# First attention: queries and keys turned unsplit in f32, two token tiles to a bank, and split behind the turn

## The chip, the cores and the metric

The kernel runs on one core of one Trainium2 chip. The metric is the device time of one execution in microseconds (us). The core has five engines with instruction queues of their own: TensorE (PE in the profile, with its weight loads as PEld), VectorE (DVE), ScalarE (ACT), GpSimd (POOL) and SyncE (SP, which issues the DMAs here). Each engine works through its queue in order; semaphores make one engine wait for another.

## The reference

The reference is a trunk of two layers over 1024 latent tokens and 256 context tokens, with a model width of 1024. Layer 0 mixes tokens by neighbourhood attention (16 heads of 64), layer 1 by sliding-window attention; each ends with a gated ConvFFN. All arithmetic is float32. Only the head of the first attention matters here, which normalises queries and keys per head:

```
y = h @ w_qkv
q = rmsnorm(y[..., :D_MODEL].reshape(bsz, t, n_kv, N_HEADS // n_kv, HEAD_DIM), g_q)
kv = y[..., D_MODEL:]
k = rmsnorm(kv[..., :kv_w].reshape(bsz, t, n_kv, HEAD_DIM), g_k)
v = kv[..., kv_w:].reshape(bsz, t, n_kv, HEAD_DIM)
...
s = jnp.einsum('...qngd,...knd->...ngqk', q, k).astype(jnp.float32) * (HEAD_DIM ** -0.5)
```

Behind it the scores get a bias (latent keys only), a softmax over latent neighbourhood and context keys together, and are multiplied by v.

## The kernel before

One program builds all stages one after another: an opening (the first modulation, the first norm, the first products with the weights), the first attention (`na`), the first ConvFFN, the sliding-window attention and the second ConvFFN. A product in f32 precision is made of f32r products: an operand is split into a high half (its rounding to f32r) and a low half (the remainder), and high x high, high x low and low x high are added up in one PSUM bank.

**The order of the work.** Each stage is planned before it is written out. `Sched.op` (line 237) records a step with its engine (or a choice of two), a planned length, what it reads and writes, a priority `key`, and which buffers it takes (`acq`) and gives back (`rel`). `Sched.run` plays the steps through in planned time, taking on each engine the ready step of lowest key; the order found is then issued, and every engine's queue stands in that order. Two tables correct the keys: `KINDS` by the name of the step, `RANKS` by its number in the plan. Waits that the plan doesn't know of are added when the steps are written out: the layer that places the semaphores makes two engines take turns on one PSUM bank, also where both only read.

**The first attention** works on eight head pairs. For each pair, `plan_na_qkv` (line 1339) is called for ten token tiles of 128 in the order 8, 9 (context) and 0 to 7 (latent). Its steps before the change, per tile:

- `plan_qkv_mm` (line 678): 24 matmuls of 384 columns (`mm<-whi,...`) give q, k and v of two heads; the first six tiles are made in the opening.
- `cp` (ACT) copies the 384 columns out of PSUM; `plan_rstd` (line 695) makes 1/rms of the four 64-wide heads, with one pow on POOL.
- `qn` (DVE) multiplies q and k by it; `qg` (POOL or DVE) multiplies q by `gg`, the product of both gains and the score's factor.
- `kd` and `qhi` (ACT) round k and q to f32r, k written twice; `klo` (DVE) and `qlo` (POOL or DVE) make the remainders. They fill a 512-column tile `st`; the k remainders go to `klt`, one for two token tiles.
- `tr` (PE) turns the four 128-column blocks of `st` in f32r into one PSUM bank of tag `pt`; `qev` (ACT), then `kev` (DVE or ACT) copy the q and the k half out. `kev` reads what `qev` wrote in the plan, so it stands behind it.
- On odd tiles `trl` (PE) turns the two blocks of `klt` into another `pt` bank, and `lev` (ACT) copies it out with two 64-partition reads.

So two token tiles take ten turns and three `pt` banks. There are two `pt` banks, used in rotation; the turns of the softmax weights (`pt<-idr,S`) take the same ones.

`plan_na_su` (line 1455) takes two query tiles of one head through scores (`s<-kkc,q`, `s<-kkl,q` and the low halves `klc`, `kll`), softmax (`S`), turns, splits (`pthi`) and the product with v (`pv<-pthi,v`). The score matmul has 128 rows: 64 of the high and 64 of the low half of q, against a k tile that holds the high half twice, plus a second k tile with the low half and 64 rows of zeros.

In the opening, `plan_quarter` (line 1101) makes a quarter of the modulation from weights `wm` that arrive by DMA (steps `mm`, `cp`, `tr`, `fin_`), and `apply` (line 1230) applies it and splits the result (`h0hi`, `h0lo`), which the first weight products wait for.

Of the kernel before, what the change touches and what calls it, by code (L numbers as in the profile page):

```python
# [38 lines left out]
class InOrder:  # L39
# [7 lines left out]
    def __getattr__(self, name):  # L47
        f = getattr(self.eng, name)

        def call(*a, **k):  # L50
# [11 lines left out]
    open=dict(load=-6, mm=1.7, tr=-9.6, fin_=0.4, sq=-9.9, v=-4.1, newton=-8.6, dg=-5.3, bc=5, lof=-6.8, mod=1.9),  # L62
    na=dict(f=0.3, cp=0.6, sq=-4.2, pw=2.2, vhi=0.2, vlo=3.3, qg=-1, kd=-0.9, qhi=-6.5, klo=0.7, qlo=-7, qev=-2, kev=-3.4,
          trl=-3.3, lev=-3.4, mm=-0.1, ctx_part=3.1, exp=0.2, hi=-0.5, lo=0.5, add=-5.5, load=-0.9, lat_part=-0.5,
          rec=2.9, ev=-0.1, scale=2.2, fin_=4.1),
# [8 lines left out]
    open={0: 0.9, 1: 21.9, 3: 18.2, 4: 28.9, 5: 11.3, 6: -19.6, 7: -0.2, 9: 3.8, 10: 1.6, 12: 31.4, 13: 32.6,  # L74
# [16 lines left out]
    na={36: 1, 47: -1.7, 48: 28.4, 50: 3, 54: 15.2, 57: 45, 61: -45.2, 62: -1.7, 67: 1.3, 68: 3.8, 69: 0.6, 71: -25,  # L91
# [304 lines left out]
def trunk_kernel(ctx, tc, xperm, xtok, xseq, cc, wmod0, wmod, bmod, gnorm, na_wqkv, na_gq, na_gk, na_bias, na_wo,  # L396
# [118 lines left out]
    def t_dve(n):  # L515
        return 0.065 + n / 960.0
# [822 lines left out]
    def plan_na_qkv(n):  # L1339
# [43 lines left out]
        def qg(e):  # L1383
            ENG[e].tensor_tensor(out=J["qn"][:, 0:2], in0=J["qn"][:, 0:2], in1=gg.unsqueeze(1).to_broadcast([P, 2, DH]),
                                 op=ALU.mult)
# [1767 lines left out]
```

## Time and profile before

| | us |
|---|---|
| median of 3 runs | 2743.69 (2743.62 to 2746.39) |
| profiled execution, its own time | 2744.96 |
| span of the profiled execution | 2743.0 |
| PE, DVE, ACT, POOL busy in the span | 2713.1, 2269.0, 1696.2, 389.3 |

The opening lasts to about 74 us, where the first turn of `st` starts; the last one of the first attention ends near 660 us, and its last head pair's softmax near 700 us. A group row names line, engine, operation, output and inputs, shapes and count, then busy time and the mean length of one in ns, then the idle time before it and what ended that. Nearly all rows carry line 51, the helper that records every instruction, so groups are told apart by the tile names. A matmul's record lasts longer than its place in the stream, since matmuls are pipelined: what one costs on PE is read from the distance between starts in the timeline.

### The profile page before, as it was taken

To read this page: it belongs to the slowest core of one execution; us is meant where nothing else is said; L and a number is where in the kernel's file an instruction comes from. 1 tells how busy PE (TensorE), PEld (TensorE's weight loads), DVE (VectorE), ACT (ScalarE), POOL (GpSimd) and SP (SyncE) were. 2 spreads that over 40 slices of the span, in tenths; PEclk is the share of its full clock that TensorE was granted. 3 is DMA by queue.
4 is the path that set the end of the run, shared out by engine and by line. 5 is a ranking of instruction groups with operands and counts; after the bars stand their busy time and mean duration, and the time that the engine had idled before them with its cause. 6 is when DMAs were issued, how large, how long until landed. Compare 5 with 4: busy or idle time off the path is not lost.

```text
span 2743.0 us, 44478 instructions
## 1 busy us (share of the span) xinstructions
PE 2713.1 (99%) x15615; PEld 2399.7 (87%) x15615; DVE 2269.0 (83%) x4860; ACT 1696.2 (62%) x3349; POOL 389.3 (14%) x649
## 2 busy tenths in 40 slices
PE   7999999999999999999999999999999999999999
PEld 6999999999899987788888889999988888888887
DVE  5878778889789677798998699888987989888766
ACT  5877777778556554455554458888864655545443
POOL 1211121224000000000000015556430000000000
PEclk9999999999999999999999999999999999999999
DMA  7233323334746544444577561010263234334745
GB/s 288 68 97 115 112 88 117 117 105 132 257 148 189 182 160 152 154 156 140 161 230 242 172 212 57 13 38 19 83 200 131 73 116 150 119 114 144 260 147 192
DMA packets 153108, 387.41 MB, mean 141 GB/s; under 512 B 23356, under 2 KB 38708, under 8 KB 151476
## 3 DMA queue, kind: packets, MB, share of 16 engines
q1 hardware_dynamic: 152884, 384.56, 43.2%
q8 instruction: 123, 2.02, 0.3%
q14 instruction: 101, 0.83, 0.1%
HBM read 313.46 MB, written 71.04 MB: 140 GB/s over the span
## 4 chain that ended last, share of the span: by engine, by line
PE 72%; DVE 2%; issue 1%; ACT 1%; DMA 0%; SPq 0%; DVEq 0%; ACTq 0%
PE ua L51 17%; PE dn L51 15%; PE uc L51 13%; PE mm L51 7%; PE ud L51 4%; PE oacc L51 4%; PE pt L51 3%; PE pv L51 3%; PE s L51 2%; PE dnc L51 2%; PE u L51 1%; PE mod L51 0%; DVE wlo L51 0%; DVE S L51 0%; PE bc L51 0%
## 5 line engine op out<-in xcount | busy, mean ns | idle before, releaser
L51 ACT ACTIVATE whi<-wraw 128x512 fp32r<-128x512 f32 (+1 forms) x264 | 213.0, 808 | 181.8 <-PE uc L51 54.3
L51 DVE TENSOR_TENSOR wlo<-wraw,whi 128x512 fp32r<-128x512 f32 (+1 forms) x264 | 240.8, 914 | 39.9 <-ACT whi L51 39.4
L51 ACT ACTIVATE S<-S,m 128x640 f32<-128x640 f32 (+3 forms) x288 | 221.0, 768 | 32.4 <-DVE m L51 25.8
L51 PE MATMUL dn<-ghi,whi 128*128 128x512 f32 x616 | 240.2, 390 | 0.0
L51 PE MATMUL dn<-ghi,wlo 128*128 128x512 f32 x616 | 240.0, 390 | 0.0
L51 PE MATMUL dn<-glo,whi 128*128 128x512 f32 x616 | 239.9, 389 | 0.0
L51 ACT ACTIVATE pthi<-pt 128x512 fp32r<-128x512 f32 (+2 forms) x384 | 195.5, 524 | 60.7 <-PE pt L51 38.3
L51 DVE SCALAR_TENSOR_TENSOR u<-c,cv,u 128x1023 f32<-128x1023 f32 x176 | 222.3, 1281 | 3.4 <-ACT u L51 2.9
L51 ACT ACTIVATE whi<-s 128x1024 fp32r<-128x1024 f32 (+1 forms) x116 | 109.0, 940 | 164.6 <-PE uc L51 111.0
L51 ACT ACTIVATE ghi<-graw 128x512 fp32r<-128x512 f32 x154 | 96.4, 630 | 176.5 <-PE dn L51 102.2
L51 PE MATMUL pt<-idr,S 128*128 128x128 f32 x1280 | 192.9, 273 | 1.6 <-DVE pthi L51 1.1
L51 PE MATMUL mm<-whi,h0hi 128*128 128x384 f32 x480 | 169.8, 354 | 0.0
L51 DVE TENSOR_TENSOR glo<-graw,ghi 128x512 fp32r<-128x512 f32 x154 | 105.6, 690 | 72.6 <-ACT ghi L51 66.9
L51 PEld LDWEIGHTS pt<-idr,S 128*128 128x128 f32 x1280 | 152.3, 141 | 13.7 <-DVE pthi L51 1.4
L51 PE MATMUL mm<-wlo,h0hi 128*128 128x384 f32 x480 | 161.7, 337 | 0.0
L51 PE MATMUL pv<-pthi,v 128*128 128x256 f32 (+1 forms) x560 | 153.2, 354 | 2.4 <-DVE pthi L51 1.5
L51 POOL TENSOR_TENSOR qy<-qv,mhalf 128x4 f32<-128x4 f32 (+1 forms) x112 | 121.3, 1084 | 210.2 <-DVE qv L51 193.2
L51 DVE TENSOR_TENSOR wlo<-s,whi 128x1024 fp32r<-128x1024 f32 (+1 forms) x116 | 124.5, 1076 | 23.0 <-ACT whi L51 22.7
L51 DVE TENSOR_TENSOR pthi<-pt,pthi 128x512 fp32r<-128x512 f32 (+2 forms) x208 | 117.9, 582 | 24.8 <-ACT pthi L51 23.0
L51 POOL TENSOR_TENSOR n1y<-n1v,mhalf 128x4 f32<-128x4 f32 (+1 forms) x8 | 8.9, 1113 | 905.8 <-DVE n1v L51 905.8
L51 PEld LDWEIGHTS dn<-ghi,whi 128*128 128x128 f32 x616 | 115.7, 188 | 24.0
L51 PEld LDWEIGHTS dn<-glo,whi 128*128 128x128 f32 x616 | 115.7, 188 | 23.9
(404 smaller groups left out, 8733.1 us busy)
## 6 DMA issues: line engine op xcount, KB each, us to landing
wraw<-in_w_up_dram SPq DMA_DIRECT2D x132, 512.0 KB, 4.2
wm<-in_wmod_dram SPq DMA_DIRECT2D x80, 512.0 KB, 3.9
wraw<-in_w_down_dram SPq DMA_DIRECT2D x44, 512.0 KB, 4.3
graw<-g_dram SPq DMA_DIRECT2D x44, 512.0 KB, 4.8
wraw<-in_w_down_dram SPq DMA_DIRECT2D x88, 256.0 KB, 3.2
graw<-g_dram SPq DMA_DIRECT2D x66, 256.0 KB, 2.9
slab<-in_na_wqkv_dram SPq DMA_DIRECT2D x32, 384.0 KB, 3.2
woraw<-in_na_wo_dram SPq DMA_DIRECT2D x24, 512.0 KB, 5.0
```

The source lines that it names most:

```text
L51: r = f(*a, **k)
```

## The change

`tr` now turns the normalised q and k themselves, in f32 and not yet split, two token tiles at once: q of both tiles in columns 0 to 255 of one `pt` bank, k of both in 256 to 511. The split is made from that bank, head by head, each step on 64 partitions and 256 columns:

- `qh` (ACT) writes the rounded q, times `gg` as a factor per partition; `ql` (DVE) writes the remainder to the other 64 partitions.
- `kh` (ACT) writes the rounded k; `kx` (ACT or POOL, SBUF to SBUF) copies it to the other 64 partitions; `kl` (DVE) writes the remainder.

The steps `qg`, `kd`, `qhi`, `klo`, `qlo`, `qev`, `kev`, `trl` and `lev` are gone, and so are the tiles `st` and `klt`. `gg` is one column. `qn` has four buffers instead of two; q tiles hold two token tiles, in half as many buffers. The gains come as one column from the host. `KINDS` and `RANKS` of the opening and of the first attention have new values; from the first ConvFFN on, the order on every engine is as it was.

```diff
-        sc.op("dve", t_dve(256), qn, reads=[K("raw"), K("y")], writes=[K("qn0"), K("qn1")], key=key,
-              acq=[("qn", K("qn"), 4)], rel=[K("raw")])
...
-            act.activation(J["kd"], J["qn"][:, 2:4].unsqueeze(2).to_broadcast([P, 2, 2, DH]), AF.Copy)
...
-            pt = J["pt"] = psa("pt", F32R)
-            for i in range(4):
-                pe.transpose(pt[:, i * P:(i + 1) * P], J["st"][:, i * P:(i + 1) * P], idr)
-        sc.op("pe", 0.35, tr, reads=[K("ql"), K("qh"), K("kd")], writes=[K("pt")], key=key, acq=[("pt", K("pt"), 2)],
-              rel=[K("st"), K("st")])
...
+        if tt % 2 == 0:
+            return
...
+            pt = J["pt"] = psa("pt", F32)
             for i in range(4):
+                src = f["qn", tt - 1 + i % 2]["qn"][:, i // 2 * 2:i // 2 * 2 + 2]
+                pe.transpose(pt[:, i * P:(i + 1) * P], src.rearrange("p h d -> p (h d)"), idf)
+        before = ("q0", hp, tt - 1)
+        sc.op("pe", 0.436, tr, reads=[K("qn"), before + ("qn",)], writes=[K("pt")], key=key, acq=[("pt", K("pt"), 8)],
+              rel=[K("qn"), before + ("qn",)])
+        for h2 in range(2):
+            r, x = ql_rows[h2], ql_rows[1 - h2]
...
+                act.activation(f["q"][pr][r, h2, :], J["pt"][r, 0:256], AF.Copy, scale=gg[r, :])
...
+                dve.scalar_tensor_tensor(out=t[x, h2, :], in0=J["pt"][r, 0:256], scalar=gg[r, :], in1=t[r, h2, :].bitcast(F32),
+                                         op0=ALU.mult, op1=ALU.subtract)
...
+                copy(e, kh_t()[r, h2, pair_cols], J["pt"][r, 256:512])
...
+                copy(e, kh_t()[x, h2, pair_cols], kh_t()[r, h2, pair_cols].bitcast(F32))
+            sc.op(("act", "pool"), (t_act(256), t_pool(256)), kx, reads=[kt("kh", h2)], writes=[kt("kx", h2)], key=key)
...
+                dve.tensor_tensor(out=kl_t()[r, h2, pair_cols], in0=J["pt"][r, 256:512],
+                                  in1=kh_t()[r, h2, pair_cols].bitcast(F32), op=ALU.subtract)
```

**On PE, in the stage's middle.** This is a piece of PE's queue before, where tiles of the second latent half (`n1lo`) are projected; `st` and `klt` are the split q and k and the k remainders:

```order
L51 MATMUL pt<-idr,st 128x128 x4
L51 MATMUL s<-kkc,q 128x256
L51 MATMUL s<-klc_697,q 128x256
L51 MATMUL s<-kkc,q 128x256
L51 MATMUL s<-klc_697,q 128x256
L51 MATMUL mm<-whi,h0hi_135 128x384
L51 MATMUL mm<-whi,n1lo 128x384
L51 MATMUL mm<-wlo,h0hi_135 128x384
L51 MATMUL pt<-idr,klt 128x128 x2
```

And this is a piece of it now, at such a place; `qn` is the normalised, unsplit q and k:

```order
L51 MATMUL pt<-idr,qn 128x128 x4
L51 MATMUL mm<-whi,h0hi_135 128x384
L51 MATMUL mm<-whi,n1lo 128x384
L51 MATMUL mm<-wlo,h0hi_135 128x384
L51 MATMUL pt<-idr,S 128x128 x4
L51 MATMUL pv<-pthi,v 128x512 x2
```

Ten turns for two token tiles have become four; over the whole program the turns of `st` fall from 496 to 176 and those of `klt` from 112 to 32 (what is left belongs to the second attention), and 160 turns of `qn` are new.

**On ACT and DVE, behind the turn.** ACT before, with buffer numbers; `pt_6154` is a bank of `st` blocks, `pt_6166` one of k remainders:

```order
L51 ACTIVATE q_6164<-pt_6154 128x256
L51 ACTIVATE kkl_694<-pt_6154 128x2x128
L51 ACTIVATE kll_695<-pt_6166 64x256 x2
L51 ACTIVATE S_6074,rs0_5578<-S_6074,m0_6075 128x640
L51 ACTIVATE st_6195<-qn_6183 128x256
```

ACT now, with the engines that each row waits for; `pt_7189` holds two token tiles:

```order
L51 ACTIVATE kkl_694<-pt_7189 64x256 [waits PE_49]
L51 ACTIVATE q_7203<-pt_7189,gg_692 64x256
L51 ACTIVATE kkl_694<-kkl_694 64x256 [waits Activation_49]
L51 ACTIVATE pthi_7212<-pt_7194 128x2x256 [waits PE_49]
L51 ACTIVATE q_7203<-pt_7189,gg_692 64x256 [waits DVE_49]
L51 ACTIVATE kkl_694<-pt_7189 64x256
```

and DVE now, on the same bank:

```order
L51 TENSOR_TENSOR kll_695<-pt_7189,kkl_694 64x256 [waits PE_49,Activation_49]
L51 SCALAR_TENSOR_TENSOR q_7203<-pt_7189,gg_692,q_7203 64x256
L51 TENSOR_SCALAR S_7223,m0_7224<-s_7207 128x256 [waits PE_49]
L51 TENSOR_TENSOR pthi_7212<-pt_7194,pthi_7212 128x2x256 [waits Activation_49]
L51 SCALAR_TENSOR_TENSOR q_7203<-pt_7189,gg_692,q_7203 64x256 [waits Activation_49]
L51 TENSOR_TENSOR kll_695<-pt_7189,kkl_694 64x256
```

The bank is now read eight times, by ACT, DVE, ACT and DVE in turn: the second q read of ACT waits for DVE's first two reads, and DVE's last two wait for it. Such a wait of ACT for DVE stands on 39 of the 40 pairs of tiles; before there was none on q.

**On DVE, in the opening.** Before, between the turned input tiles (`x_125`, from PSUM banks `nps` and `pv`) and the first high half `h0hi`; `modc` is the modulation, `wlo` a low half of the weights:

```order
L51 COPY x_125<-nps 128x512
L51 TENSOR_TENSOR wlo<-slab,whi 128x768
L51 TENSOR_TENSOR modc<-mod,bmod_t 128x2x2
L51 TENSOR_TENSOR modc<-mod,modc 128x2x2
L51 TENSOR_TENSOR modc<-mod,bmod_t 128x2x2
L51 TENSOR_TENSOR modc<-mod,modc 128x2x2
L51 SCALAR_TENSOR_TENSOR modc<-modc,gn 128x2x2
L51 TENSOR_TENSOR wlo<-slab,whi 128x768
L51 TENSOR_SCALAR x_125<-x_125,modc 128x512
L51 CAST h0hi_130<-x_125 128x512
```

And now:

```order
L51 TENSOR_TENSOR modc<-mod,bmod_t 128x2x2
L51 TENSOR_TENSOR modc<-mod,modc 128x2x2
L51 TENSOR_TENSOR modc<-mod,bmod_t 128x2x2
L51 TENSOR_TENSOR modc<-mod,modc 128x2x2
L51 SCALAR_TENSOR_TENSOR modc<-modc,gn 128x2x2
L51 TENSOR_SCALAR x_125<-x_125,modc 128x512 x2
L51 TENSOR_SCALAR x_123<-x_123,modc 128x256
L51 CAST h0hi_130<-x_125 128x512
L51 CAST h0chi<-x_123 128x256
L51 TENSOR_TENSOR h0lo_131<-x_125,h0hi_130 128x512 x2
```

One copy and two `wlo` no longer stand ahead of the first `h0hi`; the two `wlo` come behind `h0lo`.

More of the change, by code (lines that the diff above doesn't have):

```diff
@@ L61 @@
 KINDS = dict(
[L62 to L65, printed above, removed]
+    open=dict(load=-0.7, mm=-6.4, cp=0.6, tr=-3.7, fin_=-5.6, sq=4, v=-2.5, newton=4.7, dg=2.3, bc=0.5, lof=-10.6,
+          mod=-1.6),
+    na=dict(eps=-3.7, f=0.3, cp=-1, sq=-2.5, vhi=10, vlo=2.9, ql=-11.4, kl=0.1, mm=-0.1, ctx_part=5.2, exp=1.3, hi=-0.5,
+          lo=0.5, pvm=-1.3, add=-11.1, load=-1, lat_part=-0.5, rec=3.4, ev=0.1, scale=9.4),
     ffn0=dict(),
@@ L1325, in trunk_kernel @@
     F = {}
-    sc = Sched(dict(CAPS, klt=1))
+    sc = Sched(dict(CAPS, qn=4, q=4, qc=1))
     op0 = Oproj(sc, 0, 2, TC, psa, [("q0", HP - 1, tt, "acc") for tt in range(NT)],
@@ L1362, in vhi @@
             copy(e, vt[:, :, 0:DH], pair(J["raw"][:, 256:384]))
-        vk, qk = ("v", hp, tt), ("q", hp, tt)
+        vk = ("v", hp, tt)
         sees = 2 if cx else sum(1 for su in range(4) if any(tt in NA_SEES[2 * su + k] for k in range(2)))
@@ L1393, in plan_na_qkv @@
-        sc.op("act", t_act(256), kd, reads=[K("qn1")], writes=[K("kd")], key=key, acq=[("st", K("st"), 2)],
-              rel=[K("qn")])
-        def qhi(e):
-            J["qhi"] = J["st"][:, 0:384].rearrange("p (e d) -> p e d", d=192)[:, :, 0:DH]
-            act.activation(J["qhi"], J["qn"][:, 0:2], AF.Copy)
-        sc.op("act", t_act(128), qhi, reads=[K("qn0"), K("kd")], writes=[K("qh")], key=key, rel=[K("qn")])
-        kp = ("klt", hp, tt // 2)
-        def klo(e):
-            if tt % 2 == 0:
-                f["klt", tt // 2] = wk.tile([P, 2, P], F32R, tag="klt", name="klt", bufs=1)
-            ENG[e].tensor_tensor(out=pair(f["klt", tt // 2][:, tt % 2, :]), in0=J["qn"][:, 2:4],
-                                 in1=J["kd"][:, :, 0, :].bitcast(F32), op=ALU.subtract)
@@ L1407, in plan_na_qkv @@
-        sc.op("dve", t_dve(128), klo, reads=[K("qn1"), K("kd")] + ([kp] if tt % 2 else []), writes=[kp], key=key,
-              acq=[("klt", kp, 1)] if tt % 2 == 0 else (), rel=[K("qn")])
-        def qlo(e):
-            ENG[e].tensor_tensor(out=pair(J["st"][:, DH:DH + P]), in0=J["qn"][:, 0:2], in1=J["qhi"].bitcast(F32),
-                                 op=ALU.subtract)
-        sc.op(("pool", "dve"), (t_pool(128), t_dve(128)), qlo, reads=[K("qn0"), K("qh")], writes=[K("ql")], key=key,
-              rel=[K("qn")])
+        sc.op("dve", t_dve(256), qn, reads=[K("raw"), K("y")], writes=[K("qn")], key=key,
+              acq=[("qn", K("qn"), 1)], rel=[K("raw")])
@@ L1416, in tr @@
+        f["qn", tt] = J
+        if tt % 2 == 0:
+            return
+        pr = tt // 2
+        ql_rows = [slice(0, DH), slice(DH, P)]
+        q, kz = ("q", hp, pr), ("kz", hp % 2 if cx else 2)
+        kt = lambda x, e: (x + "c", hp, e) if cx else (x, pr, e)
+        pair_cols = slice(0, TC) if cx else slice(pr * TC, (pr + 1) * TC)
+        kh_t = lambda: f["kkc"] if cx else kkl
+        kl_t = lambda: klcs[hp % 2] if cx else kll
         def tr(e):
-            pt = J["pt"] = psa("pt", F32R)
+            pt = J["pt"] = psa("pt", F32)
@@ L1435, in plan_na_qkv @@
-        sc.op(("dve", "act"), (t_dve(256), t_actp(256)), kev, reads=[K("pt"), qk] + ([kk] if tt == 9 else []), writes=[kk],
-              key=key, acq=[("kkc", kk, 20)] if tt == 8 else (), rel=[K("pt")], port=False)
-        if tt % 2:
-            def trl(e):
-                pl = J["pl"] = psa("pt", F32R)
-                for i in range(2):
-                    pe.transpose(pl[:, i * P:(i + 1) * P], f["klt", tt // 2][:, i, :], idr)
-            sc.op("pe", 0.17, trl, reads=[kp], writes=[K("pl")], key=key, acq=[("pt", K("pl"), 1)], rel=[kp])
-            def lev(e):
-                f["klc"] = klcs[hp % 2]
-                dst = f["klc"] if cx else kll[:, :, (tt - 1) * P:(tt + 1) * P]
-                for e2 in range(2):
-                    copy(e, dst[e2 * DH:(e2 + 1) * DH, e2, :], J["pl"][e2 * DH:(e2 + 1) * DH, :256].bitcast(F32))
-            sc.op("act", 2 * t_actp(256), lev, reads=[K("pl"), ("kz", hp % 2 if cx else 2)], writes=[("klc", hp)] if cx else [("kl", tt - 1), ("kl", tt)],
-                  key=key, acq=[("klc", ("klc", hp), 20)] if cx else (), rel=[K("pl")])
+                src = f["qn", tt - 1 + i % 2]["qn"][:, i // 2 * 2:i // 2 * 2 + 2]
@@ L1469, in plan_na_su @@
         units = []
-        reads = [("kkc", hp), ("klc", hp)] + [("q", hp, 2 * su + k) for k in range(2)]
+        reads = [(x + "c", hp, e) for x in ("kh", "kx", "kl")] + [("q", hp, su, x, e) for x in "hl"]
         for k in range(2):
@@ L1473, in plan_na_su, with get @@
             ch = NA_SEES[tt] if tt < 8 else ()
-            def get(tt=tt, ch=ch):
-                q = f["q"][tt]
-                u = dict(q=q[:, e, :], kkc=f["kkc"][:, e, :], klc=f["klc"][:, e, :], sink=None)
+            def get(tt=tt, ch=ch, k=k):
+                q = f["q"][su][:, e, k * P:(k + 1) * P]
+                u = dict(q=q, kkc=f["kkc"][:, e, :], klc=klcs[hp % 2][:, e, :], sink=None)
                 if tt < 8:
@@ L1483, in get @@
                 return u
-            units.append(dict(nl=len(ch) * P, sink=0, get=get, rel_c=[("q", hp, tt), ("kkc", hp), ("klc", hp)],
-                              rel_l=[("q", hp, tt)],
+            units.append(dict(nl=len(ch) * P, sink=0, get=get, rel_c=[("q", hp, su), ("kkc", hp), ("klc", hp)],
+                              rel_l=[("q", hp, su)],
                               mask_key=[("bias", hp, e, (0, 0, 1, 1, 1, 1, 2, 2)[tt])] if tt < 8 else []))
-            reads += [("kk", c) for c in ch] + [("kl", c) for c in ch]
+            reads += [(x, c, e) for c in sorted({c // 2 for c in ch}) for x in ("kh", "kx", "kl")]
         def val(c):
@@ L3101, in layout @@
     rows = lambda g: np.broadcast_to(g, (P, g.shape[-1]))
-    a["na_gq"], a["na_gk"] = rows(i["na_g_q"][0]), rows(i["na_g_k"][0])
+    a["na_gq"], a["na_gk"] = [np.concatenate([g, g])[:, None] for g in (i["na_g_q"][0], i["na_g_k"][0])]
     idx = _na_bias_index()
```

52 lines of the change are left out of this document (26 added, 26 removed), and 184 rows, old and new, of tables (na, open).

## The prediction

> **What bounds the kernel now.** I first read the busy shares of the page, then a table of stretches, then PE's timeline. The first row says that PE is busy nearly all the time, but a busy PE is not yet a PE that sets the time.
>
> ```profile
> PE 2713.1 (99%) x15615; PEld 2399.7 (87%) x15615; DVE 2269.0 (83%) x4860; ACT 1696.2 (62%) x3349; POOL 389.3 (14%) x649
> ```
>
> The stretches of the opening and of the first attention show more. The columns are the stretch, its length, then the busy time of PE, PEld, DVE, ACT and POOL, the granted clock of PE, and the DMA share.
>
> ```profile
> core 0: us, PE busy (x) PEld busy (x) DVE busy (x) ACT busy (x) POOL busy (x), PEclk, DMA share, GB/s
> 28.00:33.00 5.00, 0.42 (x4) 0.22 (x3) 3.42 (x11) 3.60 (x6) 0.00 (x0) 0.77 1.04 418
> 33.00:41.00 8.00, 6.61 (x20) 6.21 (x21) 3.56 (x14) 2.44 (x5) 1.01 (x1) 0.50 1.02 424
> 41.00:75.00 34.00, 32.76 (x255) 28.76 (x255) 28.94 (x84) 20.01 (x42) 7.35 (x11) 1.00 0.45 156
> 100.00:660.00 560.00, 559.96 (x3815) 526.73 (x3814) 464.79 (x1583) 428.38 (x1138) 115.02 (x153) 1.00 0.35 107
> 660.00:700.00 40.00, 36.51 (x268) 33.29 (x267) 36.96 (x93) 33.73 (x70) 17.22 (x13) 1.00 0.61 191
> ```
>
> From 100 to 660 us, where the changed steps run, PE lacks 0.04 us of being busy throughout. DVE has 560 - 464.8 = 95 us to spare there, ACT 132 us. So PE sets the pace of this stretch: matmuls taken off its queue shorten it, as long as the others go on delivering in time. From 660 to 700 us DVE is the fuller one (37 of 40 us); no turn of q or k stands there any more.
>
> **The change part by part.** *The turns.* What a turn costs on PE is read from starts in the timeline (start, length, operation):
>
> ```profile
> 307.48 0.34 PE L51 MATMUL mm<-wlo,h0hi 128*128 128x384 f32 x1
> 307.65 0.46 PE L51 MATMUL pt<-idr,st 128*128 128x128 f32 x4
> 307.95 0.41 PE L51 MATMUL mm<-whi,h0hi 128*128 128x384 f32 x1
> 308.19 0.34 PE L51 MATMUL mm<-whi,n1lo 128*128 128x384 f32 x1
> ...
> 309.84 0.34 PE L51 MATMUL mm<-wlo,h0hi 128*128 128x384 f32 x1
> 310.02 0.28 PE L51 MATMUL pt<-idr,klt 128*128 128x128 f32 x2
> 310.13 0.41 PE L51 MATMUL mm<-whi,h0hi 128*128 128x384 f32 x1
> 310.38 0.34 PE L51 MATMUL mm<-whi,n1lo 128*128 128x384 f32 x1
> 310.56 0.34 PE L51 MATMUL mm<-wlo,h0hi 128*128 128x384 f32 x1
> 310.73 0.60 PE L51 MATMUL pt<-idr,S 128*128 128x128 f32 x4
> 311.08 0.42 PE L51 MATMUL mm<-whi,h0hi 128*128 128x384 f32 x1
> 311.34 0.34 PE L51 MATMUL mm<-whi,n1lo 128*128 128x384 f32 x1
> ```
>
> Two `mm` follow each other at 0.18 us (310.38 to 310.56). From the `mm` ahead of a group of turns to the second `mm` behind it lie two such steps and the group. Four `st` turns: 308.19 - 307.48 - 0.36 = 0.35 us. Two `klt` turns: 310.38 - 309.84 - 0.36 = 0.18 us. Four turns of `S`, which are f32 blocks of 128 x 128 as the new turns of `qn` are: 311.34 - 310.56 - 0.36 = 0.42 us. The stage has 80 tiles, so 80 groups of `st` and 40 of `klt` go, and 40 groups of `qn` come: 80 x 0.35 + 40 x 0.18 - 40 x 0.42 = 28.0 + 7.2 - 16.8 = **18.4 us less on PE**. An f32 turn is dearer than an f32r one (0.105 against 0.088 us), but there are 160 of them for 400.
>
> The records themselves last longer, 273 ns for a turn of `S`, since they overlap:
>
> ```profile
> L51 PE MATMUL pt<-idr,S 128*128 128x128 f32 x672 | 100.8, 273 | 1.1 <-DVE pthi L51 1.1
> L51 PE MATMUL pt<-idr,st 128*128 128x128 f32 x320 | 37.5, 241 | 0.0
> L51 PE MATMUL pt<-idr,klt 128*128 128x128 f32 x80 | 12.2, 234 | 0.0
> ```
>
> The Trainium skill ("TensorE: Matmul & The Clock Gate", Part 4, PE-mode transpose) gives about 275 ns for such a turn in a kernel's context, mostly access latency. The trace agrees on the record (273 ns), but its starts show that only 0.105 us of it holds the queue up. By the page's figure as a cost, 240 turns fewer would give 66 us, an estimate that I don't use.
>
> *VectorE and ScalarE.* The groups that go, and the nearest to those that come:
>
> ```profile
> L51 ACT ACTIVATE st<-qn 128x256 fp32r<-128x256 f32 x79 | 32.6, 412 | 12.8 <-DVE qn L51 11.6 <-PE pt L51 0.9
> L51 ACT ACTIVATE q<-pt 128x256 fp32r<-128x256 f32 x80 | 30.1, 378 | 17.3 <-PE pt L51 16.7
> L51 ACT ACTIVATE st<-qn 128x128 fp32r<-128x128 f32 x80 | 24.3, 304 | 1.0 <-POOL qn L51 0.4 <-DVE qn L51 0.3
> L51 ACT ACTIVATE kll<-pt 64x256 fp32r<-64x256 f32 x64 | 24.0, 374 | 2.0 <-PE pt L51 1.3
> L51 DVE TENSOR_TENSOR klt<-qn,st 128x128 fp32r<-128x128 f32 x79 | 22.8, 290 | 4.6 <-ACT st L51 3.9 <-PE pt L51 0.2
> L51 DVE TENSOR_TENSOR osb<-pv,pvup 64x256 f32<-64x256 f32 x79 | 32.7, 414 | 1.6
> L51 DVE CAST kkl<-pt 128x256 fp32r<-128x256 f32 x23 | 9.7, 423 | 7.7 <-ACT q L51 7.4
> ```
>
> DVE loses 205 passes over 128 x 128 (80 of `klt`, 68 of `qg`, 57 of `qlo`) at 0.290 us and 29 casts at 0.423 us, 71.7 us in all. It gains 160 reads of a bank on 64 partitions; the nearest row is `osb`, 0.414 us, so 66.2 us. That leaves DVE about level (-5 us). ACT loses 80 x (0.412 + 0.304), 131 bank reads of 128 x 256 (80 of q, 51 of k) at 0.378 and 80 on 64 partitions at 0.374, together 136.7 us. It gains 160 bank reads at 0.374 and 71 copies SBUF to SBUF at 0.412 at most, together 89 us: 48 us lighter. POOL loses 35 small passes and gets nine copies of `kx`, on an engine with 445 us idle of 560. None of this is on the path while PE is full, and no engine becomes fuller, so these terms count nothing.
>
> *The bank behind the turn.* Here work is added to a path. The bank is read by ACT, DVE, ACT, DVE in turn, and each waits with its own queue held up behind it: on ACT the exponentials and `pthi`, on DVE the score passes, on which the turns and `pv` of PE wait. While ACT waits, DVE makes two reads, 2 x 0.414 = 0.83 us; then DVE waits for one of ACT's, 0.374 us. Per pair of tiles at most 1.2 us is exposed, against 40 x 1.2 = 48 us in all; at least nothing is, where `kx`, `pthi` or score passes stand between. The next but one turn on PE needs this bank again, and other matmuls of PE fill that time. The `CAST kkl` row above is the nearest to such a wait: 23 such reads behind ACT's q read waited 7.4 us, 0.3 us each, and PE missed nothing by it. I take +2 us, and 0 to 16 us (0.4 us on each of 40 pairs) for the range.
>
> *The opening.* PE stands idle ahead of the first weight product:
>
> ```profile
> 33.14 0.69 PE L51 MATMUL s<-whi,h0hi 128*128 128x384 f32 x1 [4.72 <-DVE h0hi L51]
> 35.08 0.69 PE L51 MATMUL s<-whi,h0lo 128*128 128x384 f32 x1 [1.25 <-DVE h0lo L51]
> ```
>
> ```profile
> 29.73 0.96 DVE L51 TENSOR_TENSOR wlo<-slab,whi 128x768 fp32r<-128x768 f32 x1 [1.47 <-ACT whi L51]
> 30.60 0.16 DVE L51 TENSOR_TENSOR modc<-mod,bmod_t 128x4 f32<-128x4 f32 x1
> 31.33 0.96 DVE L51 TENSOR_TENSOR wlo<-slab,whi 128x768 fp32r<-128x768 f32 x1
> 32.21 0.54 DVE L51 TENSOR_SCALAR x<-x,modc 128x512 f32<-128x512 f32 x1
> ```
>
> The chain that ends in `h0hi` holds two `wlo`, each taking 0.87 us to the next start. Both move behind `h0lo`, which saves 1.7 us if the inputs of `modc` are there that early. The most is the whole idle time, 6.0 us; but the weights for the next quarter come over DMA queues that are full until 41 us (share 1.02), so PE may only wait later. If a second gap held the clock at 0.50 as from 33 to 41 us, 8 us at half speed would cost up to 4 us. I take -2.5 us, with -5 to +4 us. The small rest (which softmax passes go to ACT in the last 40 us, where DVE is full) I put at 0, with 2 us either way.
>
> *The sum.* -18.4 - 2.5 + 2.0 = -18.9 us. The profiled execution took 2744.96 us (span 2743.0 and 1.96 around it), so 2726.1 by it. It lies 1.3 us above the median of the runs, 2743.69; from that, **2724.8 us**.
>
> **The rivals.**
>
> *Part of the gain is given back at the bank* (chance 0.13). If the turns in rotation catch up with the bank, so that PE waits a further 0.25 us at each of 40 pairs, 10 us go: 2734.8. For it speaks the new taking of turns, which the plan's lengths don't hold; against it, that ACT has 48 us less to do. The Trainium skill ("PSUM — Partial Sum Buffer", PSUM bank collisions raise a hardware error) says that two engines must be kept apart on one bank and quadrant, reads against reads too: the wait can't be dropped. The casts' 7.4 us agree that one read stands behind the other.
>
> *Slower: the hand-over lands on PE in full* (0.05). If all 1.2 us per pair reach PE, +48 stands in place of +2: 2743.7 - 20.9 + 48 = 2770.8. It decides against the change from (18.4 + 2.5) / 40 = 0.52 us of PE wait per pair. DVE's 95 us and ACT's 132 us to spare speak against it.
>
> *No change* (0.07). DVE and ACT might in truth set the pace, with PE's order merely cut to it: then the freed time becomes waits of PE, 2743.7. DVE's 83% in the stretch speaks against it; that part of its idle time is waiting, which can't be filled, speaks for it.
>
> *A turn costs what its record lasts* (0.02): 320 x 0.241 + 80 x 0.234 - 160 x 0.273 = 52.2 us less, 2689 with the other terms. The starts above contradict it.
>
> That the change doesn't do what it says can't be: PE's queue holds 160 turns of `qn` and 400 turns fewer of the others.
>
> **How the numbers follow.** The forecast (PE's 18.4 us stay gained) has 0.73, and its own range is 2716 to 2732: from -18.4 - 5 - 2 with a few us for the turns' reading, to a loss of up to 8 us at the bank. The range reaches on to 2736 to take in the given-back case: 0.69 of the forecast's chance and 0.11 of that one make 0.8. A measurement of this kernel can tell 0.2%, 5.5 us, from no change. Faster by more: 0.73 + 0.13 + 0.02 = 0.88; within it 0.07; slower 0.05.
>
> **What would show it.** Right: PE still busy throughout between the first turn of `qn` and the last, with this stretch some 18 us shorter; four turns of `qn` at about 0.42 us by starts; DVE's busy time there level, ACT's some 45 us less; PE's first `h0hi` product some 2 us earlier. Wrong: waits of PE's turns for DVE `kll` or `q`, or of its score products for DVE `q`, of more than 0.4 us per pair; a second idle gap of PE ahead of 50 us with the clock at 0.5; or 64-partition reads that take much longer than 0.414 us.

## The result: slower by 0.8%

| | median of the runs | range | profiled span |
|---|---|---|---|
| before | 2743.94 us (4 runs) | 2743.62 to 2746.39 | 2743.0 us |
| changed | 2766.35 us (4 runs) | 2765.2 to 2768.1 | 2763.9 us |

The ratio is 1.0080, with a 95% interval of 1.0063 to 1.0098. The forecast was 2724.8 us in a range of 2716 to 2736; the change costs 22 us where 19 were to be gained. It came out near the rival to which I had given a chance of 0.05.

**The profile after.** The page's busy shares hardly move:

```profile
PE 2708.3 (98%) x15375; PEld 2379.5 (86%) x15375; DVE 2272.7 (82%) x4767; ACT 1685.4 (61%) x3220; POOL 381.2 (14%) x631
```

The same five stretches as before:

```profile
28.00:33.00 5.00, 3.37 (x9) 2.97 (x10) 4.93 (x10) 3.74 (x6) 0.00 (x0) 0.63 1.03 422
33.00:41.00 8.00, 7.47 (x56) 5.71 (x55) 2.95 (x11) 2.32 (x6) 1.01 (x1) 0.81 1.03 422
41.00:75.00 34.00, 32.14 (x221) 28.76 (x222) 27.42 (x75) 20.76 (x43) 8.12 (x11) 0.95 0.40 149
100.00:660.00 560.00, 537.31 (x3496) 495.51 (x3495) 449.99 (x1444) 402.14 (x987) 101.26 (x133) 1.00 0.32 102
660.00:700.00 40.00, 35.43 (x241) 31.41 (x240) 37.80 (x122) 37.18 (x80) 18.79 (x14) 1.00 0.52 157
```

From 100 to 660 us PE now stands idle for 22.7 us, where it had 0.04. DVE and ScalarE are not fuller for it: 450 and 402 of 560 us, 15 and 26 us less than before. An engine that waits while none has become fuller points to waits in a ring, not to a new bound.

To see where the 20.9 us of span came in, I take three marks on PE: the first product behind the opening, the first product of the output projection, and the rest. Before:

```profile
72.14 0.33 PE L51 MATMUL mm<-whi,h0hi 128*128 128x384 f32 x1
...
700.89 0.40 PE L51 MATMUL oacc<-o0hi,whi 128*128 128x512 f32 x1
```

After:

```profile
70.14 0.33 PE L51 MATMUL mm<-whi,h0hi 128*128 128x384 f32 x1
...
718.86 0.40 PE L51 MATMUL oacc<-o0hi,whi 128*128 128x512 f32 x1
```

The opening is 2.0 us shorter. The stage takes 648.7 us instead of 628.8, 20.0 more. What lies behind it takes 2.9 us more (2045.0 for 2042.1); in the other runs below it takes 2042.0 to 2047.5 us, in those with the kernel before 2044.5 to 2046.2, so these 2.9 us are within what executions scatter. In the stage I also took, for each operation on PE, its start to the next start, less the median of such a step before, and added up what is more than 0.25 us: 4.7 us of stops before, 40.9 after. So without stops PE's work there shrank from 624.1 to 607.8 us, 16.3 us, near the 18.4 of the forecast. How one step is matched with another moves the counts (4.6 to 9.4 us before, 39 to 45 after), but each way gives 34 to 36 us more stops and 14 to 16 us less of other work. The lighter turns brought nearly what they were to bring; the stops took more than twice that.

One such stop, on PE (start, length, operation, idle time ahead of it and what ended it):

```profile
304.60 0.66 PE L51 MATMUL pt<-idr,qn 128*128 128x128 f32 x4
...
305.85 0.60 PE L51 MATMUL pt<-idr,S 128*128 128x128 f32 x4
...
308.23 0.28 PE L51 MATMUL s<-klc,q 128*128 128x256 f32 x1
309.86 0.63 PE L51 MATMUL pt<-idr,S 128*128 128x128 f32 x4 [1.35 <-DVE kll L51]
```

The turn of `qn` at 304.60 takes one of the two `pt` banks, the turn of `S` at 305.85 the other. The next `S` turn needs the first bank back. PE has 3.7 us of other work, then waits for DVE's last read `kll`. What ScalarE and DVE did with the bank meanwhile:

```profile
305.29 0.38 ACT L51 ACTIVATE kkl<-pt 64x256 fp32r<-64x256 f32 x1 [0.74 <-PE pt L51]
305.69 0.38 ACT L51 ACTIVATE pvup<-pv 64x256 f32<-64x256 f32 x1
306.08 0.47 ACT L51 ACTIVATE q<-pt,gg 64x256 fp32r<-64x256 f32 x1
307.03 0.38 ACT L51 ACTIVATE kkl<-pt 64x256 fp32r<-64x256 f32 x1 [0.48 <-DVE kll L51]
307.44 0.47 ACT L51 ACTIVATE q<-pt,gg 64x256 fp32r<-64x256 f32 x1
```

```profile
306.58 0.42 DVE L51 TENSOR_TENSOR kll<-pt,kkl 64x256 fp32r<-64x256 f32 x1 [1.43 <-ACT q L51]
306.93 0.41 DVE L51 TENSOR_TENSOR pvup<-pv,pvup 64x256 f32<-64x256 f32 x1
307.94 0.48 DVE L51 SCALAR_TENSOR_TENSOR q<-pt,gg,q 64x256 fp32r<-64x256 f32 x1 [0.61 <-ACT q L51]
308.34 0.41 DVE L51 TENSOR_TENSOR osb<-pv,pvup 64x256 f32<-64x256 f32 x1
308.78 0.49 DVE L51 SCALAR_TENSOR_TENSOR q<-pt,gg,q 64x256 fp32r<-64x256 f32 x1
309.28 0.43 DVE L51 TENSOR_TENSOR kll<-pt,kkl 64x256 fp32r<-64x256 f32 x1
```

DVE's first `kll` needs only `kkl`, done at 305.67, yet it waits until ScalarE's `q` is done at 306.55: it waits for its turn at the bank. ScalarE in turn waits 0.48 us for that `kll`, of which it needs nothing; in the kernel's program the two reads even lie on different partitions, `kll` on the lower 64 and `kkl` on the upper. The eight reads alone take 3.5 us; from the turn's start to the end of the last read it is 5.1 us here, and 4.34 us in the median of the 40 pairs (from the timelines). In the planned times, by the lengths in the code, the median is 3.3. The order was cut to that, and every engine works its queue strictly in that order.

How often PE waited for a bank that was still being read (PE's waits, 75 to 720 us: us in total, times, longest):

```profile
PE pt L51 <- DVE kll L51: 12.9, 16, 1.3
PE pt L51 <- DVE klc L51: 3.7, 4, 1.2
...
PE pv L51 <- DVE osb L51: 3.2, 4, 1.1
...
PE pt L51 <- DVE q L51: 0.7, 1, 0.7
```

That is 17.3 of the 31 us that PE stands idle in the stage. The groups of the reads themselves, with the idle time of their engine ahead of them:

```profile
L51 DVE SCALAR_TENSOR_TENSOR q<-pt,gg,q 64x256 fp32r<-64x256 f32 x78 | 37.7, 483 | 45.5 <-ACT q L51 27.2 <-ACT kkl L51 10.3 <-PE pv L51 4.9
L51 ACT ACTIVATE q<-pt,gg 64x256 fp32r<-64x256 f32 x78 | 36.5, 467 | 16.4 <-PE pt L51 14.5 <-DVE kll L51 0.5
L51 DVE TENSOR_TENSOR kll<-pt,kkl 64x256 fp32r<-64x256 f32 x64 | 27.0, 422 | 10.4 <-ACT q L51 7.1 <-ACT kkl L51 2.4
...
L51 ACT ACTIVATE kkl<-pt 64x256 fp32r<-64x256 f32 x64 | 23.8, 372 | 15.0 <-PE pt L51 6.9 <-DVE kll L51 5.3 <-DVE q L51 1.9
```

All the reads' waits of one engine for the other come to 49.9 us on DVE and 9.7 us on ScalarE. The 0.467 against 0.372 us on ScalarE is the price of the gain `gg` as a factor per partition.

### The profile page after: what moved, and what is told of

Read it like the earlier page. It is cut to its first block, busy times and chain, and to the rows that moved or that the text cites. A ratio compares the mean times of both kernels' runs of the same rounds, so it can differ in the third digit from the quotient of the medians.

```text
span 2763.9 us, 43693 instructions
## 1 busy us (share of the span) xinstructions
PE 2708.3 (98%) x15375; PEld 2379.5 (86%) x15375; DVE 2272.7 (82%) x4767; ACT 1685.4 (61%) x3220; POOL 381.2 (14%) x631
## 4 chain that ended last, share of the span: by engine, by line
PE 73%; DVE 2%; ACT 2%; DMA 1%; issue 1%; POOL 0%; SPq 0%; DVEq 0%; POOLq 0%; ACTq 0%
PE ua L51 17%; PE dn L51 15%; PE uc L51 12%; PE mm L51 8%; PE ud L51 4%; PE oacc L51 4%; PE pt L51 3%; PE pv L51 3%; PE s L51 3%; PE dnc L51 2%; PE u L51 1%; ACT S L51 0%; PE mod L51 0%; ACT whi L51 0%; DVE S L51 0%
## 5 line engine op out<-in xcount | busy, mean ns | idle before, releaser
L51 ACT ACTIVATE S<-S,m 128x640 f32<-128x640 f32 (+4 forms) x288 | 220.9, 768 | 50.3 <-DVE m L51 43.6
L51 PEld LDWEIGHTS dn<-ghi,wlo 128*128 128x128 f32 x616 | 115.6, 188 | 23.9
```

Of the source, the lines that this page charges most:

```text
L51: r = f(*a, **k)
```

## The experiments

**Theory A**: ScalarE and DVE take turns at the bank, so it is held longer than the plan knows, and PE's turns wait. **Theory B**: the new order, not the bank, makes PE wait. **Theory C**: the reads with the gain are simply dearer than forecast.

The results in one table. The waits are sums of rows of each trace from 75 to 720 us (PE's from 72): DVE's reads or splits for ScalarE's, ScalarE's for DVE's, and PE's turns for a read of the bank. The stage is between the two marks above.

| run | median us | ratio to before (95%) | stage | DVE for ScalarE | ScalarE for DVE | PE for the bank |
|---|---|---|---|---|---|---|
| changed | 2766.35 | 1.0080 (1.0063 to 1.0098) | 648.7 | 49.9 | 9.7 | 17.3 |
| e8_low_from_sbuf | 2737.08 | 0.9975 (0.9965 to 0.9984) | 619.1 | 20.1 | 0 | 0 |
| e1_one_handover | 2750.06 | 1.0021 (1.0011 to 1.0030) | 631.5 | 18.0 | 0 | 1.1 |
| e2_copy_out | 2746.85 | 1.0012 (1.0003 to 1.0021) | 628.3 | 14.7 | 0 | 0 |
| e6_no_gain | 2756.54 | 1.0047 (1.0031 to 1.0064) | 638.2 | 47.3 | 12.1 | 10.7 |
| c1_before_no_tables | 2756.15 | 1.0046 (1.0032 to 1.0059) | 639.4 | | | |
| c2_after_no_tables | 2769.09 | 1.0089 (1.0075 to 1.0103) | 652.6 | 54.1 | 11.5 | 19.9 |
| o1_before_new_opening | 2746.06 | 1.0007 (0.9998 to 1.0016) | 629.6 | | | |
| e1t_plan_told | 2740.73 | 0.9987 (0.9977 to 0.9996) | 621.5 | 6.3 | 0 | 0.5 |
| e7_lengths_only | 2762.39 | 1.0063 (1.0049 to 1.0076) | 645.4 | 45.9 | 16.5 | 3.4 |
| b1_plan_told_new_tables | 2743.89 | 0.9996 (0.9988 to 1.0005) | 630.0 | 7.4 | 0 | 0 |
| b2_copy_out_new_tables | 2732.46 | 0.9959 (0.9945 to 0.9972) | 617.9 | 2.1 | 0 | 1.0 |
| b0_before_new_tables | 2750.66 | 1.0022 (1.0013 to 1.0031) | 633.8 | | | |

**DVE off the bank.** The high half stands in for the bank in both subtractions, so the true low halves are left out:

```diff
-  dve.scalar_tensor_tensor(out=t[x, h2, :], in0=J["pt"][r, 0:256], scalar=gg[r, :], in1=t[r, h2, :].bitcast(F32),
+  dve.scalar_tensor_tensor(out=t[x, h2, :], in0=t[r, h2, :].bitcast(F32), scalar=gg[r, :], in1=t[r, h2, :].bitcast(F32),
...
-  dve.tensor_tensor(out=kl_t()[r, h2, pair_cols], in0=J["pt"][r, 256:512],
+  dve.tensor_tensor(out=kl_t()[r, h2, pair_cols], in0=kh_t()[r, h2, pair_cols].bitcast(F32),
```

> The low halves of q and k are subtracted from the high halves in SBUF instead of from the bank, so they come out as zero: the exact products' low part is left out. Order, lengths in the plan, and number of instructions on every engine stay as in the changed kernel; only DVE no longer reads the bank, so ScalarE's four reads needn't take turns with it. Theory A (the bank is held too long by the two engines taking turns, and the next but one turn on PE waits for it): ScalarE alone is done in some 1.7 us, PE's idle time between 75 and 660 us falls from 26 us to under 8, time 2728 to 2742. Theory B (the new order of the stage makes PE wait, whatever the bank does): PE's idle time stays above 18 us, time 2758 to 2768. Theory C (the 64-partition passes with a gain are dearer than forecast, 0.467 and 0.483 us): the passes are as long as before, so 2758 to 2768 too.

Measured 2737.08 us, 29 us below the changed kernel and inside A's range. (The low half of q does not come out as zero, as I had written: the high half is multiplied by `gg` once more.) PE's and ScalarE's queues are the same operation for operation; DVE's rows:

```profile
L51 DVE SCALAR_TENSOR_TENSOR q<-q,gg 64x256 fp32r<-64x256 f32 x78 | 37.6, 482 | 17.0 <-ACT q L51 14.6
...
L51 DVE TENSOR_TENSOR kll<-kkl 64x256 fp32r<-64x256 f32 x64 | 27.0, 422 | 7.0 <-ACT kkl L51 5.5
```

Only whose bank is read differs, and 0.482 us stands where 0.483 stood. B and C can't give 29 us; A can. PE's idle time from 75 to 660 us falls from 26.3 to 5.3 us.

**One hand-over.** The four low halves depend on all four high ones:

```diff
-            sc.op("dve", t_dve(256) + 0.06, ql, reads=[K("pt"), q + ("h", h2)], writes=[q + ("l", h2)], key=key, rel=[K("pt")],
-                  port=False)
...
+            sc.op("dve", t_dve(256) + 0.06, steps[h2][1], reads=[K("pt"), q + ("h", h2)] + [q + ("h", 1), kt("kh", 0), kt("kh", 1)], writes=[q + ("l", h2)], key=key, rel=[K("pt")],
+                  port=False, rk=base + 5 * h2 + 1)
...
```

> All four of ScalarE's bank reads first, then all four of DVE's: one change of engine at the bank instead of up to seven, and the plan knows it, since each low half now depends on all four high halves. Lengths in the plan and the tables stay. Theory A: the bank is held for about 4 x 0.42 + 4 x 0.45 = 3.5 us instead of the 4.4 us seen at 305.3 to 309.7 us, near the 3.2 to 3.6 us that PE has other work for: at least half of PE's stalls go, time 2738 to 2756. Theory B: within 6 us of the changed kernel, 2760 to 2772. Theory C: the passes are as long as before, so no gain either, 2760 to 2768.

Measured 2750.06 us, inside A's range: 16 us back. But not for the reason given there. The bank is not held for a shorter time: from the turn's start to the last read's end the median is 4.59 us, against 4.34 in the changed kernel. What went is most of the waiting of one engine for the other (60 us to 18): the reads of a pair now change engine once, not three times (1.1 changes per pair for 3.1). The order on every engine is another too, since the plan holds the new dependency, and this run doesn't part the two.

**Copy the bank out.**

```diff
+  def cpo(e):
+      J["st"] = wk.tile([P, 512], F32, tag="st", name="st", bufs=2)
+      copy(e, J["st"], J["pt"])
+  sc.op("act", t_actp(512), cpo, reads=[K("pt")], writes=[K("st")], key=key, acq=[("st", K("st"), 8)], rel=[K("pt")], port=False, rk=-1)
...
-  act.activation(f["q"][pr][r, h2, :], J["pt"][r, 0:256], AF.Copy, scale=gg[r, :])
+  act.activation(f["q"][pr][r, h2, :], J["st"][r, 0:256], AF.Copy, scale=gg[r, :])
...
```

> ScalarE copies the whole bank to SBUF in one pass of 128 x 512 (0.60 us in the rows of pthi<-pt), and all eight passes of the split read the copy; 40 passes more on ScalarE, some 24 us of its 130 idle ones, and two buffers of 2 KB. Theory A: the bank is free about 1 us behind the turn, PE's waits for kll and q go, and with them 25 to 36 us: 2726 to 2744. Theory B: PE's idle time stays, 2758 to 2775. Theory C: passes are no shorter, the chain even longer by the copy: 2764 to 2785.

Measured 2746.85 us: 19.5 us back, 2.9 us above the range of A, and well below those of B and C. ScalarE pays 39 recorded copies and dearer passes behind them:

```profile
L51 ACT ACTIVATE q<-st,gg 64x256 fp32r<-64x256 f32 x78 | 39.3, 503 | 1.3
...
L51 ACT ACTIVATE st<-pt 128x512 f32<-128x512 f32 x39 | 23.3, 596 | 16.4 <-PE pt L51 15.8
```

None of PE's waits stands at the bank of the turn any more; those left are for the softmax:

```profile
PE pt L51 <- DVE pthi L51: 6.0, 5, 2.3
PE pt L51 <- ACT S L51: 4.0, 5, 2.3
```

The longer ones lie at 84 us and from 584 to 681 us; the order was made for another chain.

**Without the gain.**

```diff
-  act.activation(f["q"][pr][r, h2, :], J["pt"][r, 0:256], AF.Copy, scale=gg[r, :])
+  act.activation(f["q"][pr][r, h2, :], J["pt"][r, 0:256], AF.Copy)
...
```

> The gain gg of queries and keys is left out: q's high half is a copy without a per-partition factor, its low half a plain subtraction. Order and lengths in the plan stay. Theory C: 0.093 us less on each of two ScalarE passes and 0.06 us less on each of two DVE passes, 0.31 us per pair, nearly all of PE's 0.9 us of stall per pair hang on it being over the fill: 2738 to 2750. Theory A: the hold is shorter by 0.31 of 4.4 us, so a third of the stall at most: 2754 to 2764. Theory B: no change, 2764 to 2768.

Measured 2756.54 us, 9.8 us less, inside A's range, near its lower end. The passes shrink as foreseen:

```profile
L51 DVE TENSOR_TENSOR q<-pt,q 64x256 fp32r<-64x256 f32 x79 | 33.3, 422 | 39.1 <-ACT q L51 25.8 <-ACT kkl L51 9.6 <-ACT kkc L51 2.6
L51 ACT ACTIVATE q<-pt 64x256 fp32r<-64x256 f32 x78 | 29.4, 377 | 16.1 <-PE pt L51 14.4 <-DVE kll L51 0.5
```

That is 0.09 us on two ScalarE reads and 0.06 us on two DVE reads, 0.30 us per pair, 12 us in all, and 9.8 of them reach the end. Here a pass on an engine with 100 us to spare costs most of its length; I take it that this is because it lies in the chain. So C is true for about a quarter of the 41.5 us between the forecast and the measurement; the waits for each other (47.3 and 12.1 us) stay, and with them the rest.

**Without the tables, in both kernels.**

```diff
-  sc.rank(RANKS["na"], KINDS["na"])
+  sc.rank({}, {})
```

> The kernel before, with the two tables of the first attention's order (its kinds and its ranks) left empty, so that the planner orders by the plain due times. Control for the next run. What the tables are worth to the kernel before isn't known beforehand: estimated 0 to 40 us slower than it.

> The changed kernel with the same two tables left empty. Theory A (turns at the bank hold it longer than the plan knows): the design itself costs, whatever the order; it is not faster than c1_before_no_tables by the 18 us of its lighter turns, but between 10 us faster and 25 us slower. Theory B (the new tables are at fault): without tables on either side the change comes out some 15 to 20 us faster than c1_before_no_tables.

Measured 2756.15 and 2769.09 us: without tables the change still costs 12.9 us, inside A's range. So the chosen numbers are not what makes it slow, and B as stated is out. But the tables save 12 us in the kernel before and only 3 in the changed one: the other 9.5 of the 22 us are there because the new tables do less for this kernel than the old ones did for theirs. The sum of the forecast has no term for this.

**The opening alone.** The entries `open` of both tables, put into the kernel before:

```diff
-    open=dict(load=-6, mm=1.7, tr=-9.6, fin_=0.4, sq=-9.9, v=-4.1, newton=-8.6, dg=-5.3, bc=5, lof=-6.8, mod=1.9),
+    open=dict(load=-0.7, mm=-6.4, cp=0.6, tr=-3.7, fin_=-5.6, sq=4, v=-2.5, newton=4.7, dg=2.3, bc=0.5, lof=-10.6,
+          mod=-1.6),
...
```

> The kernel before with the changed kernel's tables of the opening alone: PE's first h0hi product comes 3.6 us earlier in the trace of the changed kernel, the first product behind the opening's end 2.0 us earlier. If the opening's gain carries to the end: 1 to 4 us less than the kernel before. If it is caught up at the full DMA queues or at the first attention's waits: within 1 us of the kernel before.

Measured 2746.06 us, ratio 1.0007 (0.9998 to 1.0016): no gain. PE's first `h0hi` product came 1.3 us earlier (31.86 for 33.14 us), the mark behind the opening at 72.06 for 72.14 us. In the other runs with this opening that mark lies between 69.4 and 71.9 us, so the 2.0 us of the changed kernel's trace are within what executions scatter; with the old opening it lies between 70.0 and 72.1.

**The plan told.** One hand-over, and the reads' lengths as measured:

```diff
-            sc.op("act", t_actp(256), qh, ...
...
+            sc.op("act", 0.49, steps[h2][0], ...
...
-            sc.op("dve", t_dve(256), kl, ...
...
+            sc.op("dve", 0.42, steps[h2][4], ...
```

> As e1_one_handover (ScalarE's four bank reads, then DVE's four), and the planner is given the lengths that the trace of the changed kernel shows for them, start to start: 0.49 and 0.40 us on ScalarE, 0.48 and 0.42 us on DVE, where it had 0.26, 0.26, 0.39 and 0.33 us. Tables as they stand. If PE's remaining 23 us of stalls in e1_one_handover are the plan's ignorance of how long the bank is held: it sets other work ahead, stalls fall under 15 us, 2736 to 2746. If PE simply has too little other work that is ready, or the tables fit the old lengths only: 2746 to 2760.

Measured 2740.73 us, as the first case expects; its stops add up to some 16 us, near the 15. The bank is held for longer than in the changed kernel, 5.17 us in the median, and the plan counted on 5.26. PE's waits for it:

```profile
PE pt L51 <- DVE kll L51: 0.5, 1, 0.5
```

So a long hold cost PE next to nothing where the order knew it.

**The lengths told, but the turns left.** The same four lengths in the changed kernel, reads in alternation as there:

```diff
-  sc.op("act", t_actp(256), qh, reads=[K("pt")] + [q + ("h", 0)] * h2, ...
+  sc.op("act", 0.49, qh, reads=[K("pt")] + [q + ("h", 0)] * h2, ...
-  sc.op("dve", t_dve(256) + 0.06, ql, reads=[K("pt"), q + ("h", h2)], ...
+  sc.op("dve", 0.48, ql, reads=[K("pt"), q + ("h", h2)], ...
```

> The changed kernel with nothing altered but four lengths in the planner: the bank reads are put at 0.49 and 0.40 us on ScalarE, 0.48 and 0.42 us on DVE, as the trace of the changed kernel shows them start to start. That the two engines take turns is still not in the plan. By the runs so far the bank is held 4.3 us from the turn's start to the last read's end where the plan counted on 3.3; with these lengths it counts on 4.1. Theory A in its new form (not the hold itself, but the part of it that the order doesn't know, stops PE): about three quarters of the unknown part is gone, stalls of 41 us fall to 15 to 25 us, time 2742 to 2752. If the turns themselves cost, whatever the plan knows: 2758 to 2768.

Measured 2762.39 us: 4 us back, where theory A expected 14 to 24. PE's waits for the bank did go, from 17.3 to 3.4 us:

```profile
PE oacc L51 <- DVE cx L51: 4.3, 1, 4.3
PE mm L51 <- DVE wlo L51: 3.7, 5, 1.0
...
PE pt L51 <- DVE kll L51: 2.2, 7, 0.7
```

Others took their place. And the two engines' waits for each other are as long as ever, 45.9 and 16.5 us:

```profile
DVE q L51 <- ACT kkl L51: 21.7, 34, 2.2
...
DVE kll L51 <- ACT q L51: 11.4, 14, 2.1
DVE q L51 <- ACT q L51: 9.9, 17, 1.9
```

While DVE waits for its turn, all that is queued behind stands. I take it that this comes out at the end of the stage, where PE is idle for 10 of 57 us and DVE busy for 52:

```profile
660.00:717.00 57.00, 46.68 (x332) 41.92 (x332) 52.44 (x138) 46.84 (x96) 16.64 (x13) 0.99 0.56 174
```

Part of the time is the clock. The same 50 us in this run and in the changed kernel:

```profile
75.00:125.00 50.00, 44.24 (x247) 40.19 (x246) 39.32 (x130) 35.00 (x88) 10.03 (x9) 0.86 0.24 77
75.00:125.00 50.00, 44.74 (x280) 39.61 (x279) 42.55 (x145) 39.50 (x98) 11.33 (x13) 1.00 0.25 77
```

PE is as busy with 247 matmuls as with 280, and its granted clock is 0.86 for 1.00. In all, the clock stands at one half for 14.1 us of this run's stage, and never in the changed kernel's; half the speed for 14.1 us is worth up to 7 us by estimate, and without it this kernel would stand near 2755 us, between the two ranges. Why the clock fell isn't shown. So the run says that the lengths alone don't bring all back, not by how much they fall short.

Beside e1_one_handover it makes a near pair: there the plan counts on 4.0 us and 4.59 come, here on 4.1 and 4.80; hold and knowledge are alike, and the kernel with one change of engine per pair is 12 us faster than the one with 3.8. Up to 7 of these may be the clock, and the two orders differ as well, so the pair alone settles little. All runs together say more: those with three to four changes per pair take 2756 to 2769 us, those with one or none 2732 to 2750.

**A new order for what was learnt.** The two tables of the first attention are chosen anew by a search over the plan's own lengths: for e1t_plan_told (b1), for e2_copy_out with its lengths told (b2), and for the kernel before (b0). In b2, against e2_copy_out:

```diff
-  sc.op("act", t_actp(512), cpo, ...
+  sc.op("act", 0.56, cpo, ...
-    na=dict(eps=-3.7, f=0.3, cp=-1, sq=-2.5, vhi=10, vlo=2.9, ql=-11.4, kl=0.1, ...
+    na={"<lambda>": -0.4, "add": -38.7, "cp": -15.7, "cpo": 6.5, "ctx_part": 14.9, "eps": -31.4, "ev": -51.7, ...
...
```

> As e1t_plan_told, with the two tables of the first attention's order chosen anew for these lengths and dependencies. The instructions are those of the changed kernel. PE's stalls in e1t_plan_told are 16 us; with an order that fits they fall to 5 to 10 us: 2729 to 2737, below the kernel before by 0.25 to 0.55%. If the stalls come from what no order can cover (DVE or ScalarE too full): no better than e1t_plan_told, 2738 to 2746.

> As e2_copy_out, with the lengths of its passes told to the planner (0.56 us for the copy, 0.47 and 0.42 us for ScalarE's passes behind it, 0.47 and 0.41 us for DVE's) and the two tables chosen anew. Its stalls of 19 us were behind pthi and S at 640 to 700 us, none at the bank of the turn. With an order that fits: 2729 to 2738, level with b1_plan_told_new_tables within 5 us; if the 40 copies' time on ScalarE or DVE's later start is what costs, it stays 5 to 12 us above b1_plan_told_new_tables.

> Control for b2_copy_out_new_tables (2732.5 us): the kernel before, with its two tables of the first attention's order chosen anew by the same search, so that both designs had the same chance at an order. If the search alone brought the gain, this comes to 2728 to 2737 as well. If the lighter turns brought it: PE has only 4.7 us of stalls to lose here, so at best 2739, and 2739 to 2748 in all.

The one-hand-over kernel does not gain by it (2743.89 us, where 2729 to 2737 stood for an order that fits; its stops grew to 22 us), so the search is no sure way to a better order. The copied-out kernel does: 2732.46 us, inside its range but 11 us below b1_plan_told_new_tables, where I expected the two within 5 us of each other. That is 0.41% below the kernel before (0.28 to 0.55%) and 1.2% below the changed one; DVE waits 2.1 us for ScalarE's parts. The kernel before loses by the same search (2750.66 us, 2.7 us above its range), so the search alone is not what brings the gain. Of all kernels here the copied-out one is the fastest: the bank is copied out once, then split from SBUF. Between the two kernels of this search it is 18 us faster, about what the turns alone were to bring; that the search served both equally well isn't shown.

## Why the prediction was wrong

- *The turns on PE, 18.4 us less*: right. Four turns of `qn` measure 324.09 - 323.31 - 0.36 = 0.42 us by starts, as forecast, and PE's work without stops is 16.3 us less (14 to 16 by the other ways of matching).

```profile
323.31 0.34 PE L51 MATMUL mm<-wlo,h0hi 128*128 128x384 f32 x1
323.48 0.60 PE L51 MATMUL pt<-idr,qn 128*128 128x128 f32 x4
323.83 0.42 PE L51 MATMUL mm<-whi,h0hi 128*128 128x384 f32 x1
324.09 0.34 PE L51 MATMUL mm<-whi,n1lo 128*128 128x384 f32 x1
```

- *The bank behind the turn, +2 us (0 to 16)*: **this step failed.** It measured 36 us of further stops, 0.9 us per pair, against at most 0.4 in the range; without DVE's reads of the bank, in the same order, 29 us of time are gone. The mechanism stood in the text, with up to 48 us, but I sized it by one row, the `CAST kkl` that stood behind ScalarE's read for 0.3 us each without harm to PE. That read changes engine once and ends the hold. Here the bank passes back and forth 3.1 times per pair, each change waits for the other engine's queue, and each wait holds up its own.
- *"The wait can't be dropped"*: this goes further than the rule that it rests on, which is by bank and quadrant. In the program of the changed kernel, in 31 of the 42 places where ScalarE waits for DVE at such a bank, and in 39 of the 82 where DVE waits for ScalarE, the read waited for lies on the other half of the 128 partitions, because the layer that places the semaphores goes by the bank alone. A run that keeps the alternation and leaves out only these waits was not made.
- *"None of this is on the path while PE is full, ... so these terms count nothing"* and *"DVE's 95 us and ACT's 132 us to spare speak against it"*: the reasoning that failed. Spare time on average did not cover a chain through two strictly ordered queues. e6_no_gain shows it: 12 us off passes of engines with time to spare brought 9.8 us.
- *The reads' lengths, 0.374 and 0.414 us*: for the k halves right (0.372 and 0.422), for the q halves short by the gain (0.467 and 0.483). The size was off by 0.3 us per pair, and by the run without the gain worth about 10 us.
- *VectorE level, ScalarE 48 us lighter*: VectorE about right, ScalarE too high. With the measured lengths DVE's new reads take 80 x 0.483 + 80 x 0.422 = 72.4 us where 66.2 were forecast, 0.7 us more than the 71.7 that it loses, instead of 5 less. ScalarE's 80 reads of q take 0.467 us for 0.374, 7.4 us more, so it is some 40 us lighter; its busy time on the page, which counts overlapping records once, falls by 10.8 us only.
- *The opening, -2.5 us*: the trace shows -2.0, but alone it brings nothing to the end.
- *The rival "slower"*: 2770.8 us by the full 1.2 us per pair; 0.9 came. Its break-even, 0.52 us of PE wait per pair, was the right one to watch. The chance of 0.05 was wrong, for the reason above. The rival "no change" named the cause nearly: "part of its idle time is waiting, which can't be filled".
- *The rival "a turn costs what its record lasts"*: with the other terms its 52.2 us give 2691 us, not 2689. The four turns at 0.42 us speak against it as before. The 275 ns that the prediction takes from the Trainium skill ("TensorE: Matmul & The Clock Gate", Part 4, PE-mode transpose) were measured there on bf16 blocks; these turns are f32.

What stays open: how much of the 29 us of e8_low_from_sbuf is the bank that comes free late, and how much the standing queues. e7_lengths_only suggests that the first alone isn't enough, but the clock blurs it.

## What to carry to other kernels

Count how often a buffer changes between two in-order engines before it is free, not only how long each holds it: here each change cost a wait that also held up what was queued behind, and an order made in advance should hold those waits. An engine's spare time covered little in such a chain; ask what is queued behind each wait. Where a bank is to be read many times by two engines, copying it out once (0.6 us) can be cheaper than sharing it, as it was here.

## What the runs showed of the hardware

- A wait row understates a stop on PE. At 309.86 us the row gives 1.35 us, but from the start ahead (308.23) it is 1.63 us where such a step takes 0.12, so 1.5 us went. In the whole stage such stops come to 40.9 us, while PE's idle time between the same two marks is 31.3 by the records.
- A factor per partition costs ScalarE 0.09 us on a read of 64 x 256: 0.467 with it, 0.377 without, in the same place. The Trainium skill ("ScalarE: Activation LUTs", What ACT_TABLE_LOAD costs) gives about 93 ns for each such operand; the trace agrees.
- The same ScalarE pass takes longer from SBUF than from the bank: 0.503 against 0.467 us with the gain. The Trainium skill ("Perfetto Trace Analysis", Optimizing Scalar/DVE Operations) gives ScalarE a higher access cost on SBUF (about 93 ns) than on PSUM (about 51 ns), 42 ns apart; the 36 ns measured here are near that.
- On DVE the source made no difference: 0.483 us from the bank and 0.482 from SBUF (e8_low_from_sbuf) for the same pass with the gain, and 0.422 us from either for the plain subtraction of k (b2_copy_out_new_tables has 0.501 and 0.435, from SBUF too; why wasn't followed). The same sentence of the Trainium skill ("Perfetto Trace Analysis", Optimizing Scalar/DVE Operations) gives DVE about 60 ns on SBUF and 125 on PSUM; these runs don't show that difference.
